# Reordering the seven block products of an FFN on one Trainium2 core: plain products first, weight sums fetched two blocks ahead, eight feature splits moved, one down block no longer halved

## The chip, the core and the metric

The kernel runs on one core of a Trainium2 chip. The core has TensorE (matrix products), VectorE and ScalarE (element-wise work), GpSimd (a few element-wise operations and some DMA issues) and SyncE, whose queue issues most DMAs. Traces abbreviate them as PE (with PEld for its weight loads), DVE, ACT, POOL and SP. Each engine has its own instruction stream; semaphores connect them. The metric is device microseconds of one execution of the whole program, the median of several runs.

## The reference, cut to what matters

The program is one layer of a streaming encoder for 512 tokens and width 1024: two parallel token mixers, cross-attention into 256 memory tokens, a SwiGLU FFN, a final RMSNorm. Only the FFN and the end are touched here:

```
gate, up = split(rmsnorm(x, norm_ffn) @ w_gate_up, (2816, 2816))
x = x + (silu(gate) * up) @ w_down
return rmsnorm(x, norm_final)
```

All data are float32. The kernel gets float32 accuracy from three products of a reduced format: an operand is split into a high part (one ScalarE copy, L111) and a low part (one VectorE subtraction, L113), and TensorE adds high·high, high·low and low·high.

## The kernel before, in words

The 2816 features are 22 blocks of 128, numbered j = 0 to 21. Blocks 0 to 2 are computed in the plain way, with two products over the full contraction of 1024 (gate, then up), 512 tokens wide. While they run, `ffn_sums` prepares for the others: it scales the input by its norm, cuts it into four quarters (contraction halves by token halves: b11, b12, b21, b22) and forms four combinations T1 to T4. Of the seven resulting activation tiles, named "11", "21", "22", "T1", "T2", "T3" and "T4", each is cut into four contraction pieces of 128 and split into high and low.

Blocks 3 to 21 are computed by `unit(j)` with seven products where the plain way has eight. The weights of gate and up make four quarters: a11 and a12 are the two contraction halves of the gate weights (one load into `raws[0]`), a22 is the second half of the up weights. Four sums of quarters are needed:

- s1 and s3 are formed by DMA: SyncE's queue loads the first half of the up weights twice (L1172), and GpSimd's queue adds a second quarter to each by an accumulating DMA (L1173, L1174).
- s2 = s1 + a11 and s4 = a12 + s2 are formed on VectorE (L1196, L1197), one after the other.

Every one of the seven weight operands goes through `quarter`: a high part by ScalarE into half of a `whi` buffer, a low part by VectorE into half of a `wlo` buffer. A product is 12 matmuls of 128x256 (four contraction pieces, three terms each), so a block is 84 matmuls. The order of the products before is a11·"11", s2·"T2", s1·"T1", s3·"T3", a12·"21", a22·"T4", s4·"22". VectorE combines the results out of PSUM by 128x256 operations (L1200 to L1217), ScalarE applies silu, and L1219 multiplies gate and up to one tile of the hidden layer.

Buffers that matter: tag "ti" has 4 tiles, "th" 4 tiles, `whi` and `wlo` 3 tiles each (two weight operands per tile), `raw` 3 tiles. Before, s1, s3 and s4 come from "ti" and s2, the gate tile `sg` and the result tile `cc` from "th".

The order of TensorE's instructions is the order in which the generators run: `drive` steps a unit by one contraction piece (three matmuls) and then steps everything in `pending`. The order on VectorE, ScalarE, GpSimd and SyncE is set at build time by a scheduler that sees program order and its own estimate of when inputs are ready; on the chip each engine then works through that fixed list.

The hidden tiles must themselves be split before the down projection (`gu_split`). Blocks 0 to 4 are split during units 10 to 14; before, the splits of blocks 5 to 21 are driven from the down stage, three of them ahead of it and the rest beside its first block. The down projection has 8 output blocks of 66 matmuls of 128x512. Before, blocks 0 to 5 are done that way; blocks 6 and 7 are done by token halves (128x256 matmuls, `wd_last`): both blocks for the left half, then both for the right half, so that the norm and the output of the left half (`final`) run beside the right half.

Of the kernel before, what the change touches and what calls it, by code (L numbers as in the profile page):

```python
# [9 lines left out]
F32R = mybir.dt.float32r  # L10
AF = mybir.ActivationFunctionType
ALU = mybir.AluOpType
# [28 lines left out]
def hybrid_block(  # L41
# [25 lines left out]
    def G(tag, name, dt=F32):  # L67
        return up.tile([P, T], dt, tag=tag, bufs=SLOTS[tag], name=nm(name))
# [6 lines left out]
    def TMP(name, tag, bufs=None, shape=(P, T), dt=F32, pool=None):  # L75
        return (pool or tp).tile(list(shape), dt, tag="t" + tag, bufs=bufs or TB[tag], name=nm(name))
# [116 lines left out]
    def wait(n):  # L193
        for _ in range(n):
            yield
# [505 lines left out]
    def seq(*gens):  # L701
        for g in gens:
            yield from g
# [410 lines left out]
    def ffn_sums():  # L1114

        for n in NB:
            B[n] = []
        for i in range(4):
            x = []
            for k in (i, i + 4):  # L1120
                t = TMP("xn", "th")
                nc.vector.scalar_tensor_tensor(out=t, in0=x3[k], scalar=gain(C_FFN, k), in1=stat["row3"],
                                               op0=ALU.mult, op1=ALU.mult)
                x.append(t)
                yield
            his = [G("a" if i < 2 else "b", "fh", F32R) for _ in range(4)]
            los = [G("a" if i < 2 else "b", "fl", F32R) for _ in range(4)]
            for at, n in enumerate(NB):
                o = lh if at % 2 == 0 else rh
                B[n].append((his[at // 2][:, o], los[at // 2][:, o]))  # L1130
# [25 lines left out]
    def quarter(src):  # L1156

        if held[1] % 2 == 0:
            held[0] = [wp.tile([P, KD, P], F32R, tag=t, bufs=3, name=nm(t)) for t in ("whi", "wlo")]
        o = slice(4 * (held[1] % 2), 4 * (held[1] % 2) + 4)  # L1160
        held[1] += 1
        hi, lo = (t[:, o, :] for t in held[0])
        split(hi, lo, src)
        return hi, lo

    def unit(j):
        raws = [wp.tile([P, KD, P], F32, tag="raw", bufs=3, name=nm("raw")) for _ in range(2)]
        a11, a12, a22 = raws[0][:, 0:4, :], raws[0][:, 4:8, :], raws[1][:, 0:4, :]
        s1, s3, s4, s2 = (TMP("fs", t).rearrange("p (k f) -> p k f", k=4) for t in ("ti", "ti", "ti", "th"))
        nc.sync.dma_start(out=raws[0], in_=w_g[j])  # L1170
        for s in (s1, s3):
            nc.sync.dma_start(out=s, in_=w_u[j][:, 0:4, :])  # L1172
        nc.gpsimd.dma_start(out=s1, in_=w_u[j][:, 4:8, :], accum_op=ALU.add)  # L1173
        nc.gpsimd.dma_start(out=s3, in_=w_g[j][:, 0:4, :], accum_op=ALU.add)  # L1174
        nc.sync.dma_start(out=a22, in_=w_u[j][:, 4:8, :])
        e, U = TMP("fe", "c"), TMP("fU", "c")
        W, sg, cc = TMP("fW", "c"), TMP("fg", "th"), TMP("fcc", "th")
        tt = nc.vector.tensor_tensor
        rot = [PM, PD, PS, PM, PD, PM, PD]

        def product(ps, w, act):
            hi, lo = w
            for k in range(4):
                xh, xl = B[act][k]
                o = ps[:, :H]
                nc.tensor.matmul(out=o, lhsT=hi[:, k, :], rhs=xh, start=k == 0, stop=False)  # L1186
                nc.tensor.matmul(out=o, lhsT=hi[:, k, :], rhs=xl, start=False, stop=False)  # L1187
                nc.tensor.matmul(out=o, lhsT=lo[:, k, :], rhs=xh, start=False, stop=k == 3)  # L1188
                yield

        def bank(i):
            return rot[i]("fp")
        p1 = bank(0)
        yield from product(p1, quarter(a11), "11")
        nc.scalar.activation(e[:, lh], p1[:, lh], AF.Copy)
        tt(out=s2, in0=s1, in1=a11, op=ALU.add)  # L1196
        tt(out=s4, in0=a12, in1=s2, op=ALU.add)  # L1197
# [8 lines left out]
        tt(out=U[:, rh], in0=U[:, lh], in1=q[:, lh], op=ALU.add)  # L1206
        tt(out=cc[:, rh], in0=W[:, lh], in1=q[:, lh], op=ALU.add)
        p = bank(4)
        yield from product(p, quarter(a12), "21")
        tt(out=e[:, lh], in0=e[:, lh], in1=p[:, lh], op=ALU.add)  # L1210
        nc.scalar.activation(sg[:, lh], e[:, lh], AF.Silu)
        p = bank(5)
        yield from product(p, quarter(a22), "T4")
# [3 lines left out]
        tt(out=W[:, lh], in0=W[:, lh], in1=p[:, lh], op=ALU.add)  # L1217
        nc.scalar.activation(sg[:, rh], W[:, lh], AF.Silu)
# [12 lines left out]
    def gu_splits(js):  # L1231
        for j in js:
            gu_split(j)
            yield
# [32 lines left out]
    def final(tok, sq):  # L1267
        yield from wait(6)
        ps = [PS("r4") for _ in range(2)]
        for i, q in enumerate([acc4[:, tok]] + sq):  # L1270
            for tt in range(2):
                nc.tensor.matmul(out=ps[tt][:, 0:1], lhsT=q[:, tt * P : tt * P + P], rhs=ones[:, 0:1],  # L1272
                                 start=(i == 0), stop=(i == 2))
        var, rs = SM("r4", 2), SM("r4", 2)
        for tt in range(2):
            nc.vector.tensor_scalar(out=var[:, tt : tt + 1], in0=ps[tt][:, 0:1], scalar1=1.0 / D, scalar2=EPS,  # L1276
                                    op0=ALU.mult, op1=ALU.add)
        nc.gpsimd.tensor_tensor(out=rs, in0=var, in1=mhalf[:, :2], op=ALU.pow)  # L1278
        yield from wait(4)
        pr = PS("row4")  # L1280
        for tt in range(2):
            nc.tensor.matmul(out=pr[:, tt * P : tt * P + P], lhsT=rs[:, tt : tt + 1].to_broadcast([P, P]), rhs=ident,  # L1282
                             start=True, stop=True)
        for i in (3, 0, 1, 2):
            x = x2t[i][:, :, tok]
            nc.vector.tensor_tensor(out=x, in0=x, in1=pr[:, :H].unsqueeze(1).to_broadcast([P, 2, H]), op=ALU.mult)  # L1286
            (nc.scalar if i in (0, 2) else nc.sync).dma_start(out=outT[i][:, :, tok], in_=x)

    wd = series(w_d, dps, gu, wd_after, range(KD - 2), kt=KF, pieces=PIECES)
    side = gu_splits(range(5, KF))  # L1290
    for _ in range(3):
        next(side)
    drive(wd[0], side=side)
    drive(*wd[1:])
    for hf in range(2):
        tok, sq = slice(hf * H, hf * H + H), []
        drive(*[(wd_last(j, tok, PM("wd"), sq), None) for j in (KD - 2, KD - 1)])
        pending.append(final(tok, sq))
    flush()

# [71 lines left out]
```

## Time and profile before

| | us |
|---|---|
| median of 3 runs | 1235.74 (1234.57 to 1238.3) |
| the profiled execution, its time | 1235.55 |
| the profiled execution, first to last instruction (span) | 1233.8 |
| TensorE busy | 1202.9 (97% of the span) |
| VectorE busy | 765.7 (62%) |
| ScalarE busy | 585.4 (47%) |

The span is what the trace shows; the time of the same execution is 1.75 us longer, and all sums are made on the span. In a row of the timeline the first number is the start in us from the span's start, the second the duration; what stands in brackets is the engine's idle time before that row and the instruction that ended it. In a row of the windows the first number behind the stretch is its length, then the busy time of PE, PEld, DVE, ACT and POOL with the count of instructions, the clock granted to TensorE as a share of full speed, the DMA share and GB/s.

### The profile page before, as it was taken

How to read it: one execution, taken by the hardware profiler on the slowest of the kernel's cores; microseconds unless marked ns; L12 is line 12 of the kernel's file. 1: busy time of each engine (PE TensorE's matmuls, PEld its weight loads, DVE VectorE, ACT ScalarE, POOL GpSimd, SP SyncE). 2: the span in 40 equal slices, each digit the busy share in tenths (PEclk: the TensorE clock that was granted, in tenths of full speed). 3: DMA queues.
4: the chain of work that ended last, by engine and by line, in shares of the span. 5: the costliest groups of instructions: out<-in, count | busy, mean ns of one | idle time of the engine just before them, and what ended most of it. 6: DMA issues, size and time to landing. Idle time of an engine off the chain costs nothing. (4 is left out here: it accounts for less than half of the span.)

```text
span 1233.8 us, 19731 instructions
## 1 busy us (share of the span) xinstructions
PE 1202.9 (97%) x7571; PEld 1051.2 (85%) x7571; DVE 765.7 (62%) x1564; ACT 585.4 (47%) x1207; POOL 143.5 (12%) x143
## 2 busy tenths in 40 slices
PE   8999999999999999999999999999989989999997
PEld 8888887899998887777788998888789989988887
DVE  5967872356543488775365564455978878892234
ACT  7573333365741377665324443443544545462332
POOL 0022230220110000000022200003011111100000
PEclk9999998999999999999999999999989999999999
DMA  7253342211343432233324462113167766743343
GB/s 277 87 180 105 118 125 82 94 53 61 112 135 131 162 111 77 86 96 103 120 86 138 138 211 89 66 48 107 43 154 184 185 163 172 181 130 99 94 120 120
DMA packets 73053, 149.28 MB, mean 121 GB/s; under 512 B 19040, under 2 KB 27648, under 8 KB 72960
## 3 DMA queue, kind: packets, MB, share of 16 engines
q1 hardware_dynamic: 66400, 137.02, 34.2%
q0 software_dynamic: 5472, 9.96, 5.0%
q8 instruction: 59, 0.97, 0.3%
q10 hardware_dynamic: 1088, 1.05, 0.2%
q14 instruction: 34, 0.28, 0.1%
HBM read 140.13 MB, written 7.88 MB: 120 GB/s over the span
## 5 line engine op out<-in xcount | busy, mean ns | idle before, releaser
L111 ACT ACTIVATE whi<-raw 128x1024 fp32r<-128x1024 f32 (+4 forms) x224 | 206.4, 926 | 309.8 <-PE g L138 80.8
L113 DVE TENSOR_TENSOR wlo<-raw,whi 128x1024 fp32r<-128x1024 f32 (+4 forms) x210 | 228.5, 1092 | 154.6 <-ACT whi L111 152.5
L1188 PE MATMUL fp<-fh,wlo 128*128 128x256 f32 x532 | 152.9, 287 | 3.9 <-DVE wlo L113 3.9
L1186 PE MATMUL fp<-fh,whi 128*128 128x256 f32 x532 | 152.5, 287 | 3.5 <-ACT whi L111 3.2
L1187 PE MATMUL fp<-fl,whi 128*128 128x256 f32 x532 | 152.1, 286 | 2.0 <-DVE fl L113 2.0
L1188 PEld LDWEIGHTS fp<-fh,wlo 128*128 128x128 f32 x532 | 103.7, 195 | 5.1 <-DVE wlo L113 4.8
L1186 PEld LDWEIGHTS fp<-fh,whi 128*128 128x128 f32 x532 | 103.8, 195 | 4.1 <-ACT whi L111 3.6
L1187 PEld LDWEIGHTS fp<-fl,whi 128*128 128x128 f32 x532 | 103.8, 195 | 2.3 <-DVE fl L113 2.2
L111 ACT ACTIVATE whi<-fs 128x512 fp32r<-128x512 f32 x76 | 46.7, 627 | 63.5 <-PE fp L1187 46.3
L203 POOL TENSOR_TENSOR acc<-acc,sq 128x512 f32<-128x512 f32 x19 | 31.1, 1635 | 264.2 <-issue 159.7
L162 PE MATMUL nat<-whi,hh 128*128 128x256 f32 x192 | 58.8, 306 | 0.4 <-DVE conv L391 0.4
L163 PE MATMUL nat<-whi,hl 128*128 128x256 f32 x192 | 54.9, 286 | 0.0
L164 PE MATMUL nat<-wlo,hh 128*128 128x256 f32 x192 | 54.9, 286 | 0.0
L113 DVE TENSOR_TENSOR wlo<-fs,whi 128x512 fp32r<-128x512 f32 x76 | 51.3, 686 | 5.7 <-ACT whi L111 5.3
L138 PE MATMUL g<-gul,whi 128*128 128x512 f32 x132 | 51.8, 393 | 1.9 <-DVE gul L113 1.9
L139 PE MATMUL g<-guh,wlo 128*128 128x512 f32 x132 | 51.5, 390 | 0.0
L137 PE MATMUL g<-guh,whi 128*128 128x512 f32 x132 | 51.5, 390 | 0.0
L799 ACT ACTIVATE P<-P,mx 128x128 f32<-128x128 f32 (+1 forms) x64 | 35.8, 559 | 28.7 <-DVE mx L797 28.5
L113 POOL TENSOR_TENSOR wlo<-raw,whi 128x1024 fp32r<-128x1024 f32 x14 | 34.0, 2428 | 111.3 <-ACT whi L111 111.3
L162 PEld LDWEIGHTS nat<-whi,hh 128*128 128x128 f32 x192 | 37.4, 195 | 1.5 <-issue 0.6
L1173 POOL DMA_DIRECT2D fs<-in_w_u x19 | 16.7, 877 | 181.8 <-DVE wlo L113 82.2
L163 PEld LDWEIGHTS nat<-whi,hl 128*128 128x128 f32 x192 | 37.5, 195 | 0.0
(416 smaller groups left out, 3328.3 us busy)
## 6 DMA issues: line engine op xcount, KB each, us to landing
raw<-in_w_g SPq DMA_DIRECT2D x22, 512.0 KB, 5.7
raw<-in_w_d SPq DMA_DIRECT2D x20, 512.0 KB, 3.5
fs<-in_w_u SPq DMA_DIRECT2D x38, 256.0 KB, 3.7
fs<-in_w_u POOLq DMA_DIRECT2D x19, 256.0 KB, 4.0
fs<-in_w_g POOLq DMA_DIRECT2D x19, 256.0 KB, 6.3
raw<-in_w_u SPq DMA_DIRECT2D x19, 256.0 KB, 4.2
raw<-in_wk SPq DMA_DIRECT2D x8, 512.0 KB, 3.9
raw<-in_wga SPq DMA_DIRECT2D x8, 512.0 KB, 3.5
```

The costliest lines, as they stand in the source:

```text
L111: nc.scalar.activation(hi, src, AF.Copy, scale=1.0 if scale is None else scale)
L113: (eng or nc.vector).tensor_tensor(out=lo, in0=src, in1=hi.bitcast(F32), op=ALU.subtract)
L137: nc.tensor.matmul(out=ps[:, :w], lhsT=hi[:, k - a, :], rhs=xh[:, n], start=first, stop=False)
L138: nc.tensor.matmul(out=ps[:, :w], lhsT=hi[:, k - a, :], rhs=xl[:, n], start=False, stop=False)
L139: nc.tensor.matmul(out=ps[:, :w], lhsT=lo[:, k - a, :], rhs=xh[:, n], start=False, stop=last)
L162: nc.tensor.matmul(out=o, lhsT=xh[:, tok], rhs=hi[:, kw, :], start=(k == 0), stop=False)
L163: nc.tensor.matmul(out=o, lhsT=xl[:, tok], rhs=hi[:, kw, :], start=False, stop=False)
L164: nc.tensor.matmul(out=o, lhsT=xh[:, tok], rhs=lo[:, kw, :], start=False, stop=(k == KD - 1))
L799: nc.scalar.activation(pr, pr, AF.Exp, scale=-1.0, bias=mx, accum_out=rs[:, t : t + 1])
L1186: nc.tensor.matmul(out=o, lhsT=hi[:, k, :], rhs=xh, start=k == 0, stop=False)
L1187: nc.tensor.matmul(out=o, lhsT=hi[:, k, :], rhs=xl, start=False, stop=False)
L1188: nc.tensor.matmul(out=o, lhsT=lo[:, k, :], rhs=xh, start=False, stop=k == 3)
```

## The change

1. In `ffn_sums` the same 32 tiles are allocated in another order (all four contraction pieces of "11" and "21" first, then of "22" and "T1", then the rest), so that tag "a" holds the operands of "11", "21", "22" and "T1".
2. In `unit`, s1 and s3 alone stay in "ti" (two tiles of four per block), s2 and s4 both come from "th".
3. The order of the products becomes a11·"11", a12·"21", s4·"22", s2·"T2", s1·"T1", s3·"T3", a22·"T4". The combining operations are rearranged with it: gate left is now e + product "21" straight into `sg` (L1200 of the new file), and s2 and s4 (now L1202, L1203) are written in the program behind it.
4. The splits of hidden blocks 5 to 12 run inside the last unit; only blocks 13 to 21 remain beside the first down block.
5. Down block 6 is done 512 tokens wide like blocks 0 to 5; only block 7 is halved.

```
         for i in range(4):
...
-            his = [G("a" if i < 2 else "b", "fh", F32R) for _ in range(4)]
-            los = [G("a" if i < 2 else "b", "fl", F32R) for _ in range(4)]
             for at, n in enumerate(NB):
                 o = lh if at % 2 == 0 else rh
-                B[n].append((his[at // 2][:, o], los[at // 2][:, o]))
+                B[n].append([t[:, o] for t in tiles[i, at // 2]])
...
-        s1, s3, s4, s2 = (TMP("fs", t).rearrange("p (k f) -> p k f", k=4) for t in ("ti", "ti", "ti", "th"))
+        s1, s3, s2, s4 = (TMP("fs", t).rearrange("p (k f) -> p k f", k=4) for t in ("ti", "ti", "th", "th"))
...
-        p1 = bank(0)
-        yield from product(p1, quarter(a11), "11")
-        nc.scalar.activation(e[:, lh], p1[:, lh], AF.Copy)
+        p = bank(0)
+        yield from product(p, quarter(a11), "11")
+        nc.scalar.activation(e[:, lh], p[:, lh], AF.Copy)
+        p = bank(1)
+        yield from product(p, quarter(a12), "21")
+        tt(out=sg[:, lh], in0=e[:, lh], in1=p[:, lh], op=ALU.add)
+        nc.scalar.activation(sg[:, lh], sg[:, lh], AF.Silu)
         tt(out=s2, in0=s1, in1=a11, op=ALU.add)
         tt(out=s4, in0=a12, in1=s2, op=ALU.add)
-        p = bank(1)
+        q = bank(2)
+        yield from product(q, quarter(s4), "22")
+        p = bank(3)
         yield from product(p, quarter(s2), "T2")
         tt(out=U[:, lh], in0=e[:, lh], in1=p[:, lh], op=ALU.add)
-        p = bank(2)
+        p = bank(4)
         yield from product(p, quarter(s1), "T1")
         tt(out=W[:, lh], in0=U[:, lh], in1=p[:, lh], op=ALU.add)
-        q = bank(3)
-        yield from product(q, quarter(s3), "T3")
...
-        p = bank(4)
-        yield from product(p, quarter(a12), "21")
...
+        tt(out=sg[:, rh], in0=W[:, lh], in1=q[:, lh], op=ALU.add)
+        nc.scalar.activation(sg[:, rh], sg[:, rh], AF.Silu)
         p = bank(5)
+        yield from product(p, quarter(s3), "T3")
...
+        p = bank(6)
         yield from product(p, quarter(a22), "T4")
         tt(out=cc[:, lh], in0=U[:, rh], in1=p[:, lh], op=ALU.add)
-        p = bank(6)
-        yield from product(p, quarter(s4), "22")
...
         if 9 <= j < 14:
             pending.append(seq(wait(8), gu_splits([j - 9])))
+        if j == KF - 2:
+            pending.append(seq(wait(10), gu_splits(range(5, 9)), wait(8), gu_splits(range(9, 13))))
...
-    wd = series(w_d, dps, gu, wd_after, range(KD - 2), kt=KF, pieces=PIECES)
-    side = gu_splits(range(5, KF))
-    for _ in range(3):
-        next(side)
+    wd = series(w_d, dps, gu, wd_after, range(KD - 1), kt=KF, pieces=PIECES)
+    side = gu_splits(range(13, KF))
...
-        drive(*[(wd_last(j, tok, PM("wd"), sq), None) for j in (KD - 2, KD - 1)])
+        drive(*[(wd_last(j, tok, PM("wd"), sq), None) for j in (KD - 1,)])
```

The build puts VectorE's instructions in the following order. First VectorE before, from the fifth product of block 4 to the second product of block 5. Here fs_9204 and fs_9205 are s1 and s3 of block 5, fs_9207 and fs_9206 its s2 and s4, raw_9202 its gate weights; wlo rows are low parts, each waiting for its high part from ScalarE.

```order
L1210 TENSOR_TENSOR fe_9072<-fe_9072,fp_9148 128x256 [waits PE_49]
L1196 TENSOR_TENSOR fs_9207<-fs_9204,raw_9202 128x512 [waits DMASW4_49]
L113 TENSOR_TENSOR wlo_9257<-fs_9204,whi_9256 128x512 [waits Activation_49]
L113 TENSOR_TENSOR wlo_9257<-fs_9205,whi_9256 128x512 [waits DMASW5_49,Activation_49]
L1197 TENSOR_TENSOR fs_9206<-raw_9202,fs_9207 128x512 [waits DVE_49]
L1214 TENSOR_TENSOR fcc_9076<-fU_9073,fp_9165 128x256 [waits PE_49]
L113 TENSOR_TENSOR wlo_9221<-fs_9207,whi_9220 128x512 [waits Activation_49]
L1217 TENSOR_TENSOR fW_9074<-fW_9074,fp_9183 128x256 [waits PE_49]
L113 TENSOR_TENSOR wlo_9292<-raw_9202,whi_9291 128x512 [waits Activation_49]
L113 TENSOR_TENSOR wlo_9292<-raw_9203,whi_9291 128x512 [waits DMAHW1_49,Activation_49]
L1219 SCALAR_TENSOR_TENSOR gu_9200<-fcc_9076,fg_9075 128x512 [waits Activation_49]
L1200 TENSOR_TENSOR fU_9215<-fe_9214,fp_9239 128x256 [waits PE_49]
```

Before, both sums of block 5 and the low part of s2 stand ahead of the last products of block 4 being combined. Now the same place in the changed kernel, from the end of block 4 into block 5: fs_9204 is s1 of block 5, fs_9206 and fs_9207 are its s2 and s4, fp_9237 is its product "21".

```order
L1220 TENSOR_TENSOR fcc_9076<-fU_9073,fp_9184 128x256 [waits DVE_49,PE_49]
L1221 SCALAR_TENSOR_TENSOR gu_9200<-fcc_9076,fg_9075 128x512 [waits DVE_49,Activation_49]
L1200 TENSOR_TENSOR fg_9217<-fe_9214,fp_9237 128x256 [waits PE_49,Activation_49]
L1202 TENSOR_TENSOR fs_9206<-fs_9204,raw_9202 128x512 [waits DMASW4_49]
L1203 TENSOR_TENSOR fs_9207<-raw_9202,fs_9206 128x512 [waits DVE_49]
L113 TENSOR_TENSOR wlo_9258<-fs_9206,whi_9257 128x512 [waits Activation_49]
L113 TENSOR_TENSOR wlo_9258<-fs_9207,whi_9257 128x512 [waits Activation_49]
L113 TENSOR_TENSOR wlo_9291<-fs_9204,whi_9290 128x512 [waits Activation_49]
```

The two sums now stand behind L1200, which waits for TensorE's product "21" of the same block. This is the order in all odd blocks from 5 to 21 (in block 21 with splits of hidden tiles in between). In the even blocks from 4 to 20 the low part of s4 stands further back; here block 4, where fs_9064 and fs_9065 are s2 and s4, fs_9063 is s3 and raw_9061 holds a22:

```order
L1200 TENSOR_TENSOR fg_9075<-fe_9072,fp_9093 128x256 [waits PE_49,Activation_49]
L1202 TENSOR_TENSOR fs_9064<-fs_9062,raw_9060 128x512
L1203 TENSOR_TENSOR fs_9065<-raw_9060,fs_9064 128x512 [waits DVE_49]
L113 TENSOR_TENSOR wlo_9131<-fs_9064,whi_9130 128x512 [waits Activation_49]
L113 TENSOR_TENSOR wlo_9167<-fs_9063,whi_9166 128x512 [waits DMASW3_49,Activation_49]
L113 TENSOR_TENSOR wlo_9167<-raw_9061,whi_9166 128x512 [waits DMAHW5_49,Activation_49]
L113 TENSOR_TENSOR wlo_9095<-fs_9065,whi_9094 128x512 [waits Activation_49]
```

Three other low parts now stand between s4 and its own low part. TensorE in the same block, from the last matmul of product "21" (fp_9093) into product "22" (fp_9114), whose weights are the halves of whi_9094 and wlo_9095 that hold s4:

```order
L1190 MATMUL fp_9093<-fh_8637,wlo_9095 128x256
L1188 MATMUL fp_9114<-fh_8639,whi_9094 128x256 [waits PE_49,Activation_49]
L1189 MATMUL fp_9114<-fl_8640,whi_9094 128x256
L1190 MATMUL fp_9114<-fh_8639,wlo_9095 128x256 [waits DVE_49]
L1188 MATMUL fp_9114<-fh_8641,whi_9094 128x256
```

The product with s4 was the seventh of a block and is now the third; its first matmul waits for ScalarE's high part, its third for VectorE's low part.

More of the change, by code (lines that the diff above doesn't have):

```diff
@@ L1117, in ffn_sums @@
             B[n] = []
+        tiles = {}
+        for at in range(4):
+            for i in range(4):
+                tiles[i, at] = [G("a" if at < 2 else "b", n, F32R) for n in ("fh", "fl")]
         for i in range(4):
@@ L1192, in bank @@
             return rot[i]("fp")
-        p1 = bank(0)
-        yield from product(p1, quarter(a11), "11")
-        nc.scalar.activation(e[:, lh], p1[:, lh], AF.Copy)
+        p = bank(0)
[5 more added lines that the diff above has]
+        nc.scalar.activation(sg[:, lh], sg[:, lh], AF.Silu)
         tt(out=s2, in0=s1, in1=a11, op=ALU.add)
         tt(out=s4, in0=a12, in1=s2, op=ALU.add)
-        p = bank(1)
+        q = bank(2)
+        yield from product(q, quarter(s4), "22")
+        p = bank(3)
         yield from product(p, quarter(s2), "T2")
         tt(out=U[:, lh], in0=e[:, lh], in1=p[:, lh], op=ALU.add)
-        p = bank(2)
+        p = bank(4)
         yield from product(p, quarter(s1), "T1")
         tt(out=W[:, lh], in0=U[:, lh], in1=p[:, lh], op=ALU.add)
-        q = bank(3)
-        yield from product(q, quarter(s3), "T3")
-        tt(out=U[:, rh], in0=U[:, lh], in1=q[:, lh], op=ALU.add)
-        tt(out=cc[:, rh], in0=W[:, lh], in1=q[:, lh], op=ALU.add)
-        p = bank(4)
-        yield from product(p, quarter(a12), "21")
-        tt(out=e[:, lh], in0=e[:, lh], in1=p[:, lh], op=ALU.add)
-        nc.scalar.activation(sg[:, lh], e[:, lh], AF.Silu)
+        tt(out=sg[:, rh], in0=W[:, lh], in1=q[:, lh], op=ALU.add)
+        nc.scalar.activation(sg[:, rh], sg[:, rh], AF.Silu)
         p = bank(5)
+        yield from product(p, quarter(s3), "T3")
+        tt(out=U[:, rh], in0=U[:, lh], in1=p[:, lh], op=ALU.add)
+        tt(out=cc[:, rh], in0=W[:, lh], in1=p[:, lh], op=ALU.add)
+        p = bank(6)
         yield from product(p, quarter(a22), "T4")
         tt(out=cc[:, lh], in0=U[:, rh], in1=p[:, lh], op=ALU.add)
-        p = bank(6)
-        yield from product(p, quarter(s4), "22")
-        tt(out=W[:, lh], in0=W[:, lh], in1=p[:, lh], op=ALU.add)
-        nc.scalar.activation(sg[:, rh], W[:, lh], AF.Silu)
         nc.vector.scalar_tensor_tensor(out=gu_tile(), in0=cc, scalar=-1.0, in1=sg, op0=ALU.mult, op1=ALU.mult)
@@ L1272, in final @@
                 nc.tensor.matmul(out=ps[tt][:, 0:1], lhsT=q[:, tt * P : tt * P + P], rhs=ones[:, 0:1],
-                                 start=(i == 0), stop=(i == 2))
+                                 start=(i == 0), stop=(i == len(sq)))
         var, rs = SM("r4", 2), SM("r4", 2)
```

## The prediction, made before the changed kernel ran

> **What bounds the kernel now.** I read the page first, then TensorE's waits, then the FFN by windows and, where it loses time, row by row.
>
> ```profile
> span 1233.8 us, 19731 instructions
> PE 1202.9 (97%) x7571; PEld 1051.2 (85%) x7571; DVE 765.7 (62%) x1564; ACT 585.4 (47%) x1207; POOL 143.5 (12%) x143
> ```
>
> TensorE is busy nearly throughout, so the time is its work plus its waits. Its longest waits over the whole span:
>
> ```profile
> PE fp L1188 <- DVE wlo L113: 3.9, 4, 1.9
> PE fp L1186 <- ACT whi L111: 3.2, 2, 2.0
> PE fp L1187 <- DVE fl L113: 2.0, 1, 2.0
> PE g L138 <- DVE gul L113: 1.9, 3, 1.4
> ```
>
> The first three are the seven-product units (fp), the fourth is the way into the down stage. The units from their first matmul to the first of the down stage:
>
> ```profile
> 890.65 0.28 PE L1186 MATMUL fp<-fh,whi 128*128 128x256 f32 x1
> ...
> 1097.62 0.39 PE L137 MATMUL g<-guh,whi 128*128 128x512 f32 x1
> ```
>
> That is 206.97 us for 19 blocks. In steady running a matmul starts every 0.12 us (the first two rows of the next fence), so a block needs 84 x 0.12 = 10.08 and 19 need 191.5. The units lose 15.45 us in all. One of the two places where they lose it shows how:
>
> ```profile
> 1002.38 0.28 PE L1187 MATMUL fp<-fl,whi 128*128 128x256 f32 x1
> 1002.50 0.28 PE L1188 MATMUL fp<-fh,wlo 128*128 128x256 f32 x1
> 1003.97 0.39 PE L1186 MATMUL fp<-fh,whi 128*128 128x256 f32 x1 [1.18 <-ACT whi L111]
> 1004.19 0.28 PE L1187 MATMUL fp<-fl,whi 128*128 128x256 f32 x1
> 1006.37 0.58 PE L1188 MATMUL fp<-fh,wlo 128*128 128x256 f32 x1 [1.91 <-DVE wlo L113]
> ...
> 1001.96 0.69 DVE L113 TENSOR_TENSOR wlo<-fs,whi 128x512 fp32r<-128x512 f32 x1 [2.21 <-ACT whi L111]
> 1002.57 0.68 DVE L1196 TENSOR_TENSOR fs<-fs,raw 128x512 f32<-128x512 f32 x1
> ...
> 1004.43 1.29 DVE L113 TENSOR_TENSOR wlo<-raw,whi 128x512 fp32r<-128x512 f32 x2
> 1005.64 0.68 DVE L113 TENSOR_TENSOR wlo<-fs,whi 128x512 fp32r<-128x512 f32 x1
> ...
> 1003.28 0.63 ACT L111 ACTIVATE whi<-fs 128x512 fp32r<-128x512 f32 x1
> ```
>
> VectorE stood 2.21 us at one instruction, and the sum s2 (L1196) queued behind it came late. Then everything went in a chain: sum 1002.57 to 1003.25, high part on ScalarE 1003.28 to 1003.91, first matmul 1003.97; the low part had to wait for two others and ended at 1006.32, third matmul 1006.37. The engine takes its list in order. Behind the stall TensorE's granted clock is 0.50:
>
> ```profile
> 896.80:903.60 6.80, 5.31 (x23) 5.01 (x24) 4.28 (x10) 1.69 (x4) 1.81 (x2) 0.50 0.65 166
> 1006.10:1009.40 3.30, 3.03 (x14) 3.03 (x15) 1.24 (x4) 0.70 (x2) 0.86 (x1) 0.50 1.04 301
> ```
>
> From 1006.37 to 1009.40, 14 matmuls took 3.03 us instead of 14 x 0.12 = 1.68: the half clock cost another 1.35. At the start of the units it lasted 6.8 us, twice as long, so up to 3.4.
>
> **The change, term by term.** *The third product.* By the order on VectorE, s2 and s4 now stand behind L1200, which needs the block's product "21", and TensorE's very next product needs s4. Nothing covers this chain: TensorE's list has no other product to go on with. (Before, the sums stood three or more products ahead.) The pieces of the chain, beside those above:
>
> ```profile
> 905.12 0.28 PE L1188 MATMUL fp<-fh,wlo 128*128 128x256 f32 x1
> ...
> 905.44 0.42 DVE L1206 TENSOR_TENSOR fU<-fU,fp 128x256 f32<-128x256 f32 x1 [1.01 <-PE fp L1188]
> 905.78 0.42 DVE L1207 TENSOR_TENSOR fcc<-fW,fp 128x256 f32<-128x256 f32 x1
> ...
> 990.21 0.69 DVE L1196 TENSOR_TENSOR fs<-fs,raw 128x512 f32<-128x512 f32 x1
> 990.93 0.69 DVE L1197 TENSOR_TENSOR fs<-raw,fs 128x512 f32<-128x512 f32 x1
> ...
> 907.94 1.15 ACT L111 ACTIVATE whi<-fs 128x512 fp32r<-128x512 f32 x2
> 909.00 0.62 ACT L111 ACTIVATE whi<-raw 128x512 fp32r<-128x512 f32 x1
> ```
>
> From the start of a product's last matmul to the VectorE operation that reads it is 0.32 (905.12 to 905.44), the next operation follows 0.34 later, s4 follows s2 by 0.72, high parts follow each other by 0.53, low parts by 0.60 (1004.43 to 1005.64 for two). Count from the start of the last matmul of "21":
>
> - Odd blocks: L1200 at 0.32, s2 at 0.66, s4 at 1.38 to 2.07; its high part 2.10 to 2.73, TensorE's first matmul at 2.79. The low part of s2 at 2.04, that of s4 when its high part is there, 2.76 to 3.45; third matmul 3.50. Without a wait it would be at 3 x 0.12 = 0.36: 3.14 us lost.
> - Even blocks: the low parts of s2, s3, a22 at 2.04, 2.64, 3.24, that of s4 at 3.84 to 4.53 (its high part, fourth on ScalarE from 1.38, is there at 3.60); third matmul 4.58: 4.22 lost.
> - Block 21: the splits of three hidden tiles stand between; s4 at 2.46, its low part 4.26 to 4.95: 4.64 lost.
> - Block 3: "11" and "21" are covered better than before, but behind L1200 stand three rows of `ffn_sums`, then s2, another such row, s4 and two low parts: 0.34 x 4 to s2, 0.94 to s4, 1.38 to the start of its low part, 0.69, 0.05, so 4.4 from L1200, which VectorE reaches some 0.8 late because it still works through the last pieces: 5.2 lost.
>
> Sum of the stalls: 9 x 4.22 + 8 x 3.14 + 4.64 + 5.2 = 72.9. The bounds are narrow, since every piece has a row: about 62 if the low part of s4 were always next in turn (18 x 3.14 and 5.2), 80 with another 0.4 of waiting in each block.
>
> *The half clock.* Each of the 19 stalls is like the one at 1002.5, whose two idle pieces (1.18 and 1.91, with two matmuls between) were enough. Bounds: nothing, or 3.2 each (nearly the 6.8 us stretch). I take 1.6, near the 1.35 of the same kind of stall, a little up because the even blocks' stalls are longer: 30.4. The units then lose 72.9 + 30.4 = 103.3 where they lost 15.45: **+87.9**.
>
> The Trainium skill, page "TensorE: Matmul & The Clock Gate", section "HAM oscillation — how this bites in real kernels", gives the rule that only gaps in TensorE's work of over some 3.4 us bring it back to half speed. By that rule hardly any of the new stalls would, since the longest unbroken idle piece is about 3.4 (even blocks, 0.28 to 3.65); the trace differs, since at 1002.5 no idle piece was over 1.91 and the clock still fell to 0.50, and I go by the trace. The rule makes the second rival below.
>
> *Weight sums two blocks ahead* (s1 and s3 use half of "ti" each block). This removes what made VectorE stand at 1001.96; what it gains lies within the 15.45 already taken off. The two extra loads and two accumulating DMAs that now go out early (about 720 us) pass SyncE's and GpSimd's queues, which have room:
>
> ```profile
> 900.12 0.92 POOL L1173 DMA_DIRECT2D fs<-in_w_u  x1 [37.80 <-DMA fs<-in_w_u]
> ```
>
> GpSimd stood idle 37.8 us ahead of its next sum. Cost zero; if that cover were gone the first blocks would start some us later. All later loads have more time than before, since a block takes 15 us.
>
> *Eight splits in block 21.* Three of them lengthen its stall (counted). The rest runs beside its last five products, so the 1.9 us in front of the down stage (the row of g L138) goes: **-1.9**, from 0 to -2.7.
>
> *Down block 6 whole.*
>
> ```profile
> 1130.60 0.69 DVE L1254 TENSOR_TENSOR x<-g,x 128x512 f32<-128x512 f32 x1 [1.99 <-PE g L139]
> 1145.63 0.69 DVE L1254 TENSOR_TENSOR x<-g,x 128x512 f32<-128x512 f32 x1 [1.99 <-PE g L139]
> ...
> 1208.96 1.25 PE r L1272 x12
> ```
>
> A whole block takes 15.03; 132 matmuls of 256 columns at 0.12 take 15.8, so 0.75 is saved, and 4 of the 12 small matmuls of the first half's norm (1.25 us in the row), 0.25 on average of what they cost. The left half's norm now has 7.9 us of block 7 as cover instead of 15.8 and needs about 5 until its outputs are issued. **-1.0**, from -1.2 to +2 if those outputs hold up the last ones.
>
> **Sum.** 1233.8 + 87.9 - 1.9 - 1.0 = 1318.8 for the span, and 1.75 more for the execution's time as before (1235.55 against 1233.8; the median of the runs, 1235.74, is the same within 0.2): **1320 us**.
>
> **The rivals.**
>
> 1. *Two half-clock stretches per stall.* The half clock begins late in a stall, finds little work in its first stretch and stays, as at 896.8. For it: the even blocks' stalls of over 4 us. Against it: the one stall of the same kind had one stretch. 19 x 3.2 = 60.8 in place of 30.4: 1351.
> 2. *No half clock.* Then 30.4 less: 1290. The row of clock 0.50 behind 1006.37 speaks against it.
> 3. *Faster: VectorE gets to the sums in time.* The mechanism would be that VectorE starts L1202 and L1203 while L1200 still waits for "21"; it decides from the point where both sums are ready 2.1 us ahead of the end of "21". Then the unit's waits go nearly all (2 us at the start stay): 1235.55 - 13.4 - 1.9 - 1.0 = 1219. The inputs are there, thanks to the earlier fetch. Against it: at 1001.96 VectorE stood 2.21 us with the sum behind it and did not take it.
> 4. *The change doesn't do what it says*: the fetch ahead is nullified because s2 and s4 share four "th" tiles with `sg` and `cc`, and gain and loss cancel. Only a cost of stalls near 18 us, one us per block, would do that, a third of the shortest chain.
>
> **Chances.** Forecast (1300 to 1340) 0.62; rival 1 0.15; rival 2 0.14; rival 3 0.06; rival 4 or otherwise within the noise 0.02; slower by a few us for other reasons 0.01. A measurement here can tell 0.3% (3.7 us). Faster by more: 0.06; within: 0.02; slower: 0.92. The range takes in rivals 1 and 2, whose bounds are those of the half clock: 1287 to 1353.
>
> **What would show it.** TensorE's waits "fp <- ACT whi" and "fp <- DVE wlo" with about 18 entries each, some 2.5 to 3.4 and 0.4 to 0.8 us long; blocks 10.1 us long before, alternately about 15 and 16 now; L1200 waiting on TensorE in every block and L1202 right behind it; clock segments of 0.50 in every block, 3.4 us each; the first g matmul some 88 us later than 1097.6; the down stage 3 us shorter. The forecast is wrong if L1202 starts ahead of L1200's product, or if the granted clock stays at 1 through the units.

## The result: 1322.68 us, and the profile after

The changed kernel takes 1322.68 us (median of 4 runs, 1320.84 to 1325.7) against 1236.03 for the kernel before: a ratio of 1.0684, 95% interval 1.0638 to 1.073. The profiled execution has a span of 1319.8 us, where 1318.8 had been worked out. Ratios, here and in the table of the experiments, leave out one run, of 1233.53 us in the row "the same again", which was over 1.5% above the fastest of its kernel.

The head of the page, after:

```profile
span 1319.8 us, 19554 instructions
PE 1235.9 (94%) x7497; PEld 1075.6 (81%) x7497; DVE 772.0 (58%) x1560; ACT 585.2 (44%) x1202; POOL 144.9 (11%) x144
```

TensorE has 74 instructions fewer and shows 33 us more busy time: the same matmuls took longer, for the most part because of the half clock. Its longest waits (waited for: total, times, longest):

```profile
PE fp L1188 <- ACT whi L111: 59.3, 19, 4.4
PE fp L1190 <- DVE wlo L113: 4.2, 14, 0.5
```

There are 19 waits for 19 units, all at the first matmul of the third product. The two stages by windows (length, then busy time of PE, PEld, DVE, ACT, POOL, granted clock, DMA share, GB/s):

```profile
889.22:1186.80 297.58, 233.77 (x1598) 225.03 (x1597) 184.78 (x342) 107.98 (x209) 29.45 (x34) 0.86 0.46 112
1186.80:1319.80 133.00, 124.58 (x620) 105.69 (x618) 48.38 (x63) 40.71 (x53) 9.15 (x8) 0.97 0.34 102
```

The units take 297.6 us instead of 207.0, the down stage 133.0 instead of 136.2, and the units begin 1.4 us earlier: 90.6 - 3.2 - 1.4 = 86.0, the difference of the spans. One odd block (9), TensorE, VectorE and ScalarE from the timeline:

```profile
988.08 0.28 PE L1190 MATMUL fp<-fh,wlo 128*128 128x256 f32 x1
990.93 0.39 PE L1188 MATMUL fp<-fh,whi 128*128 128x256 f32 x1 [2.57 <-ACT whi L111]
991.15 0.38 PE L1189 MATMUL fp<-fl,whi 128*128 128x256 f32 x1
991.66 0.58 PE L1190 MATMUL fp<-fh,wlo 128*128 128x256 f32 x1
...
988.47 0.42 DVE L1200 TENSOR_TENSOR fg<-fe,fp 128x256 f32<-128x256 f32 x1 [1.73 <-PE fp L1190]
988.81 0.68 DVE L1202 TENSOR_TENSOR fs<-fs,raw 128x512 f32<-128x512 f32 x1
989.53 0.69 DVE L1203 TENSOR_TENSOR fs<-raw,fs 128x512 f32<-128x512 f32 x1
990.19 2.62 DVE L113 TENSOR_TENSOR wlo<-fs,whi 128x512 fp32r<-128x512 f32 x4
...
989.53 2.40 ACT L111 ACTIVATE whi<-fs 128x512 fp32r<-128x512 f32 x4 [0.18 <-DVE fs L1202]
```

VectorE stands 1.73 us at L1200 until product "21" is out, and only then come s2 and s4; TensorE waits 2.57 us for the high part of s4. In the even blocks the splits stand in another order; block 10:

```profile
1002.75 0.28 PE L1190 MATMUL fp<-fh,wlo 128*128 128x256 f32 x1
1006.43 0.38 PE L1188 MATMUL fp<-fh,whi 128*128 128x256 f32 x1 [3.41 <-ACT whi L111]
...
1007.40 0.39 PE L1190 MATMUL fp<-fh,wlo 128*128 128x256 f32 x1 [0.47 <-DVE wlo L113]
...
1004.85 1.29 DVE L113 TENSOR_TENSOR wlo<-fs,whi 128x512 fp32r<-128x512 f32 x2
1006.07 0.68 DVE L113 TENSOR_TENSOR wlo<-raw,whi 128x512 fp32r<-128x512 f32 x1
1006.67 0.68 DVE L113 TENSOR_TENSOR wlo<-fs,whi 128x512 fp32r<-128x512 f32 x1
...
1004.19 1.15 ACT L111 ACTIVATE whi<-fs 128x512 fp32r<-128x512 f32 x2 [0.19 <-DVE fs L1202]
1005.25 0.61 ACT L111 ACTIVATE whi<-raw 128x512 fp32r<-128x512 f32 x1
1005.77 0.61 ACT L111 ACTIVATE whi<-fs 128x512 fp32r<-128x512 f32 x1
```

Three high parts (s2, s3, a22) stand on ScalarE ahead of that of s4, and three low parts on VectorE.

To split the 297.6, take the prediction's own measure of a stall: from the start of the last matmul of "21" to the start of the third of "22", less the 0.36 that this takes without a wait. Over the 19 blocks it comes to 74.2, and another 0.3 is lost in block 3 ahead of "21". Behind the third matmul of "22" a block has 58 matmuls left, 6.96 us at 0.12; together they take 31.5 more than that. Not all of this is the half clock: in the run with 24 matmuls in each stall (below), where one stretch of half clock is left, the 18 blocks without it take 7.05 for this part, 0.09 more than 6.96, or 1.8 over 19 blocks. So the stalls cost 74.2 + 0.3 + 1.8 = 76.3 and the half clock 29.7, and 191.5 + 76.3 + 29.7 is the 297.6 of the row but for rounding.

| term (us on the span) | predicted | measured |
|---|---|---|
| stalls at the third product | 72.9 | 76.3 |
| half clock behind them | 30.4 (19 stalls of 1.6) | 29.7 (13 stalls with one stretch, 1.36 each; 6 with two, 2.0 each) |
| losses of before that go | -15.45 | -15.5 |
| down stage | -2.9 | -3.2 |
| start of the units | 0 | -1.4 |
| sum | +85.0 | +86.0 (difference of the spans) |

### The profile page after: what moved, and what is told of

It reads as the page before. It is cut to its first block, busy times and chain, and to the rows that moved or that the text cites. A ratio compares the mean times of both kernels' runs of the same rounds, so it can differ in the third digit from the quotient of the medians.

```text
span 1319.8 us, 19554 instructions
## 1 busy us (share of the span) xinstructions
PE 1235.9 (94%) x7497; PEld 1075.6 (81%) x7497; DVE 772.0 (58%) x1560; ACT 585.2 (44%) x1202; POOL 144.9 (11%) x144
## 5 line engine op out<-in xcount | busy, mean ns | idle before, releaser
L113 DVE TENSOR_TENSOR wlo<-raw,whi 128x1024 fp32r<-128x1024 f32 (+4 forms) x207 | 224.4, 1092 | 177.2 <-ACT whi L111 174.2
L1188 PE MATMUL fp<-fh,whi 128*128 128x256 f32 x532 | 167.4, 315 | 59.3 <-ACT whi L111 59.3
L1190 PE MATMUL fp<-fh,wlo 128*128 128x256 f32 x532 | 167.5, 315 | 4.4 <-DVE wlo L113 4.2
L1188 PEld LDWEIGHTS fp<-fh,whi 128*128 128x128 f32 x532 | 117.6, 221 | 63.2 <-ACT whi L111 63.2
L1189 PE MATMUL fp<-fl,whi 128*128 128x256 f32 x532 | 164.7, 310 | 0.0
L1190 PEld LDWEIGHTS fp<-fh,wlo 128*128 128x128 f32 x532 | 116.7, 219 | 9.1 <-DVE wlo L113 9.1
L1189 PEld LDWEIGHTS fp<-fl,whi 128*128 128x128 f32 x532 | 117.1, 220 | 0.3 <-DVE fl L113 0.2
L138 PE MATMUL g<-gul,whi 128*128 128x512 f32 x154 | 60.1, 390 | 0.0
L139 PE MATMUL g<-guh,wlo 128*128 128x512 f32 x154 | 60.1, 390 | 0.0
L137 PE MATMUL g<-guh,whi 128*128 128x512 f32 x154 | 60.1, 390 | 0.0
```

The source lines that it names most:

```text
L113: (eng or nc.vector).tensor_tensor(out=lo, in0=src, in1=hi.bitcast(F32), op=ALU.subtract)
L137: nc.tensor.matmul(out=ps[:, :w], lhsT=hi[:, k - a, :], rhs=xh[:, n], start=first, stop=False)
L138: nc.tensor.matmul(out=ps[:, :w], lhsT=hi[:, k - a, :], rhs=xl[:, n], start=False, stop=False)
L139: nc.tensor.matmul(out=ps[:, :w], lhsT=lo[:, k - a, :], rhs=xh[:, n], start=False, stop=last)
```

## The experiments

Units means the time from the first matmul of unit 3 to the first of the down stage, from the profiled execution of each run. "Stalls" and "other excess" are a plain count over all successive matmuls of the units: what the time from one start to the next has over 0.12 us, added up for those over 0.4 us (stalls) and for the others. The others are the half clock and intervals of about 0.22 right behind a stall. All time comparisons are with runs of the kernel before on the same chip.

| kernel | time, us | ratio to before (95%) | units | stalls | other excess |
|---|---|---|---|---|---|
| before | 1236.03 | | 207.0 | 10.9 | 4.6 |
| changed | 1322.68 | 1.068 (1.064 to 1.073) | 297.6 | 70.3 | 35.7 |
| sums written first | 1252.52 | 1.010 (1.005 to 1.016) | 225.7 | 23.4 | 10.8 |
| old product order | 1228.05 | 0.992 (0.990 to 0.995) | 202.4 | 8.1 | 2.7 |
| "22" last | 1297.68 | 1.043 (1.031 to 1.056) | 264.3 | 49.2 | 23.6 |
| 18 matmuls in each stall | 1300.77 | 1.052 (1.045 to 1.059) | 275.0 | 31.0 + 41.0 filled | 11.5 |
| 24 matmuls in each stall | 1298.03 | 1.046 (1.031 to 1.061) | 269.5 | 18.6 + 54.7 filled | 4.7 |
| before, two ahead only | 1230.46 (one run) | | 201.6 | 7.1 | 3.0 |
| "T1" third, "T2" fourth | 1221.62 | 0.988 (0.982 to 0.994) | 195.0 | 3.3 | 0.2 |
| the same again | 1224.79 | 0.982 (0.973 to 0.991) | 195.0 | 3.3 | 0.2 |
| "T2" third, "T1" fourth | 1220.95 | 0.982 (0.975 to 0.989) | 194.7 | 2.8 | 0.3 |

### The sums written first

```
+        tt(out=s2, in0=s1, in1=a11, op=ALU.add)
+        tt(out=s4, in0=a12, in1=s2, op=ALU.add)
         p = bank(0)
         yield from product(p, quarter(a11), "11")
...
         nc.scalar.activation(sg[:, lh], sg[:, lh], AF.Silu)
-        tt(out=s2, in0=s1, in1=a11, op=ALU.add)
-        tt(out=s4, in0=a12, in1=s2, op=ALU.add)
```

> The changed kernel, but the two weight sums s2 and s4 are written in the program at the head of the unit instead of behind the combination with product "21". Products, buffers, splits and the down stage stay. By the build's order the sums then stand among the last combinations of the block before; in the odd blocks the low part of s4 is also ahead of L1202 (the combination with "21"), in the even blocks its high part is still fifth on ScalarE behind the high parts of s3 and a22, which wait for a buffer that product "11" frees, and its low part stands behind L1202. Theory A (the sums' place behind the combination makes the stalls): odd blocks lose at most 0.3 us, even blocks about 1.6 (first matmul of "22" 0.9 late, third another 0.6), the clock stays at 1 in most blocks; units 213 us instead of 297.6, time 1237. Rival B (product "22" is late because its inputs arrive late by DMA or because its splits take their time, wherever the sums stand): stalls of about 3 us stay in every block, time above 1290.

Two lines in another place take 70 us off. Most odd blocks lose 0.05 to 0.07 us, most even ones about 2.0, so rival B falls: the inputs and the splits are early enough where the list lets them. VectorE in block 8 (even):

```profile
957.24 0.69 DVE L1196 TENSOR_TENSOR fs<-raw,fs 128x512 f32<-128x512 f32 x1
...
960.25 0.42 DVE L1202 TENSOR_TENSOR fg<-fe,fp 128x256 f32<-128x256 f32 x1
960.58 0.68 DVE L113 TENSOR_TENSOR wlo<-fs,whi 128x512 fp32r<-128x512 f32 x1
```

s4 is ready at 957.93, its low part still stands behind L1202. The time was missed by 15 us: block 3 loses 7.6, even blocks 2.0 instead of 1.6, blocks 10 to 12 another 5 (in block 12 a split of a hidden tile stands between L1202 and the low part of s4), and the clock falls in blocks 3, 4, 6 and 12.

### The old order of products

The unit's body is that of the kernel before, the operand tiles are named in its order ("11", "T2", "T1", "T3", "21", "T4", "22"); the rest is the changed kernel.

> The changed kernel with the unit's products in the order of before ("11", "T2", "T1", "T3", "21", "T4", "22") and the operand tiles named in that order; s1 and s3 two blocks ahead, the eight splits in block 21 and the whole down block 6 stay. Theory A (only the place of the sums and of product "22" costs): the units keep the loss at their start (about 9.5 us) and lose the stall at block 13, 202 us; the way into the down stage and the down stage stay as in the changed kernel (133.0 us from the first g matmul to the end); time 1227, faster than before by about 9. Rival B (the fetch ahead, with half of the ti tiles, or the splits in block 21 cost time themselves): the units take 207 or more and the time is 1235 or above.

202.4 and 1228.05, as theory A had it: 17 of the 19 blocks take 10.08 us. So nothing but the order of products and sums makes the changed kernel slower.

### "22" last, the sums where they are

```
-        q = bank(2)
-        yield from product(q, quarter(s4), "22")
-        p = bank(3)
+        p = bank(2)
         yield from product(p, quarter(s2), "T2")
...
+        p = bank(6)
+        yield from product(p, quarter(s4), "22")
```

> The changed kernel with only product "22" moved from third to last place (operand tiles named in that order); the sums stay behind the combination with "21". The third product is now "T2", whose weights s2 are one sum behind the combination where s4 was two. Theory A (a sum written behind the combination of the second product stalls the product that needs it by the length of its chain): from the last matmul of "21", L1200 at 0.32, s2 0.66 to 1.35, its high part to 2.01, first matmul of "T2" at 2.07; s4 stands between s2 and the low part, which ends at 2.72, third matmul 2.77; 2.4 us lost in every block, odd and even alike, and the clock falls in most of them for 1.4 more: blocks of 12.5 to 14 us, units 235 to 262, time 1258 to 1285. Rival (only the two sums of s4 one after the other are too long, a single sum is hidden): blocks of 10.1 to 10.5, units 195 to 203, time 1219 to 1227.

The stall moved to the new third product, and is as long as its shorter chain (block 9):

```profile
977.43 0.28 PE L1190 MATMUL fp<-fh,wlo 128*128 128x256 f32 x1
979.55 0.38 PE L1188 MATMUL fp<-fh,whi 128*128 128x256 f32 x1 [1.85 <-ACT whi L111]
...
977.81 0.42 DVE L1200 TENSOR_TENSOR fg<-fe,fp 128x256 f32<-128x256 f32 x1 [1.35 <-PE fp L1190]
978.15 0.68 DVE L1202 TENSOR_TENSOR fs<-fs,raw 128x512 f32<-128x512 f32 x1
```

First matmul at 2.12 (2.07 expected), 2.4 to 2.6 us lost in most blocks. The units came out just above the upper end (264.3 against 262): blocks 3 and 21 lose over 6 us each. The time did not: the two runs took 1288.51 (the profiled one) and 1306.85, 3.5 and 22 us above the upper end. The mean granted clock of the slower one was 0.959 against 0.976, so it had more half clock; it has no trace that shows where. The rival falls: one sum behind the combination is enough.

### Matmuls that fill the stall

```
+        wt = quarter(a12)
-        yield from product(p, quarter(a12), "21")
+        yield from product(p, wt, "21")
...
         q = bank(2)
+        for _ in range(18):
+            nc.tensor.matmul(out=q[:, :H], lhsT=wt[0][:, 0, :], rhs=B["21"][0][0], start=True, stop=True)
         yield from product(q, quarter(s4), "22")
```

> The changed kernel with 18 extra matmuls of 128x256 between products "21" and "22" of every unit (high part of a12 times the first piece of "21", into the PSUM bank that product "22" then starts afresh), so that TensorE works 18 x 0.12 = 2.2 us of each stall. They end before the first weights of s4 are there (2.85 us after the last matmul of "21" in odd blocks, 3.69 in even ones), so the stalls themselves stay. Theory A (the stalls bring the half clock, and it costs 35.7 us): the stretches of clock 0.50 in the units go from 19 to 3 or fewer, the units shrink from 297.6 to about 263 us, time 1288. Rival (the half clock is not set off by idle time of this length, or costs nothing because the following products have room): time 1320 or, with the extra work on the path, above.

342 extra matmuls make the kernel 22 us faster than the changed one. The stalls are as long as ever: in every block the third matmul of "22" starts as far behind the last of "21" as in the changed kernel, within 0.02 us. The clock is at 0.97 over the units:

```profile
889.92:1164.96 275.04, 249.88 (x1939) 241.93 (x1938) 184.34 (x343) 108.15 (x209) 29.45 (x34) 0.97 0.50 121
```

The units were missed by 12 us for two reasons. Five stretches were left where at most 3 had been expected; they cost 7.1 us behind the third matmuls. And the 263 had put the whole "other excess" of 35.7 down to the clock, of which some 6 belong to the stalls. The same with `range(24)`:

> As the run with 18 extra matmuls per unit, but with 24 (2.9 us of TensorE work in each stall). Theory A (a stretch of 3.41 us in which TensorE works less than about half is followed by half clock): with 18, six stretches fell, all behind a window with a busy share of 0.49 or less; with 24 the idle left is 0 to 0.5 in odd blocks and 0.7 plus 0.6 in even ones, so no window but those of blocks 3 and 21 comes below 0.6, and at most 2 stretches of half clock are left. The stalls stay 72 us (filled or not), the units come to 191.5 + 72 + 1 to 4 = 265 to 268 us instead of 275, the time to 1290 to 1293. Rival (the half clock comes from something else in these blocks, such as the change of products): 5 or more stretches again, time near 1300 or above.

(The "six stretches" of this text were five.) One stretch is left in the units:

```profile
895.24:1164.75 269.51, 255.68 (x2054) 249.37 (x2052) 184.07 (x342) 108.18 (x209) 29.48 (x34) 0.99 0.51 124
901.56:904.97 3.41, 1.79 (x13) 1.59 (x13) 3.31 (x7) 3.10 (x6) 0.00 (x0) 1.00 0.23 77
904.98:908.39 3.41, 3.41 (x19) 3.41 (x18) 1.66 (x4) 0.64 (x2) 0.92 (x1) 0.50 0.88 252
```

The second row is the emptiest window, the third the half clock behind it. Block 10, with the extra matmuls between the first two rows:

```profile
998.62 0.28 PE L1190 MATMUL fp<-fh,wlo 128*128 128x256 f32 x1
1002.31 0.39 PE L1188 MATMUL fp<-fh,whi 128*128 128x256 f32 x1 [0.54 <-ACT whi L111]
1002.53 0.28 PE L1189 MATMUL fp<-fl,whi 128*128 128x256 f32 x1
1003.28 0.39 PE L1190 MATMUL fp<-fh,wlo 128*128 128x256 f32 x1 [0.47 <-DVE wlo L113]
```

The third matmul of "22" starts 4.66 behind the last of "21", where it took 4.65 without the filling. So the filling leaves the stall as it is and takes away what stood behind it: the units are 28.1 us shorter than the changed kernel's, though they hold 456 matmuls more. The stretch that is left costs about 1.5 us, and 28.1 + 1.5 is the price of the half clock that was given above; it is the same comparison, not a second one. The time did not follow all the way (1298.03, not 1290 to 1293): the units began at 895.2, 6 us late, for the reason in the last section.

### Two ahead alone, in the kernel before

```
-        s1, s3, s4, s2 = (TMP("fs", t) ... for t in ("ti", "ti", "ti", "th"))
+        s1, s3, s2, s4 = (TMP("fs", t) ... for t in ("ti", "ti", "th", "th"))
```

> The kernel before with one edit alone: s1 and s3 come from ti, s2 and s4 from th, so the weight sums by DMA are fetched two blocks ahead. Products, splits and the down stage are those of before. Theory A (the loss at block 13 came from a DMA sum that was late): the loss at the start of the units stays (about 9 us), that at block 13 (4.95 us) shrinks to 1.5 or nothing, those at blocks 5 and 15 go; units 201 to 203 us instead of 207, the down stage 136.2 us as before. Rival (the fetch ahead takes something from the blocks, since s4 now shares four th tiles with s2, the gate tile and the result tile): blocks over 10.1 us in the whole stage, units 207 or more.

Theory A: block 13 loses 1.5 instead of 4.95, blocks 5 and 15 nothing. This edit is worth 5.3 us of the units; in the changed kernel it can't be seen beside the stalls.

### Versions that are faster than both

The plain halves lead, the sums are written at the head of the unit, and the product with s4 is last. First with "T1" third:

```
         p = bank(2)
         yield from product(p, quarter(s1), "T1")
         tt(out=W[:, lh], in0=e[:, lh], in1=p[:, lh], op=ALU.add)
         p = bank(3)
         yield from product(p, quarter(s2), "T2")
         tt(out=U[:, lh], in0=e[:, lh], in1=p[:, lh], op=ALU.add)
         tt(out=W[:, lh], in0=W[:, lh], in1=p[:, lh], op=ALU.add)
...
         p = bank(6)
         yield from product(p, quarter(s4), "22")
```

> The changed kernel with the products in the order "11", "21", "T1", "T2", "T3", "T4", "22": the plain halves still lead, then the two products whose weights need no VectorE sum or only s2, and "22" with s4 last; the sums are written at the head of the unit; one more combination of 128x256 per block on VectorE. By the build's order every low part stands well ahead of its product. Theory A: all blocks from 4 on take 10.1 us, block 3 between 11 and 16; units 193 to 198 us, first g matmul near 1085, time 1217 to 1222, faster than before by some 15 us. Rival B (it is not the place of the sums but VectorE's load, with the extra operation, or the early leading halves that hold the units back): blocks of 11 us and more, time 1235 or above.

> The version with "T1" third and "T2" fourth once more, beside the one above on the same chip: units 195 us, time 1219 to 1224, faster than before by 12 to 16 us. If the gain were an accident of the earlier runs, the two would come out at the time of before.

Then with "T2" third, so that W = U + "T1" as before and the additional operation goes:

> As the version with "T1" third and "T2" fourth, but "T2" third and "T1" fourth, which saves the additional combination per block on VectorE; sums at the head of the unit. Theory A: in the build's order the low part of s2 stands ahead of the block's combination with "21" in odd and even blocks, so blocks of 10.1 us from 4 on; block 3 needs s2 two products earlier than there, while VectorE still works through the last pieces of the input, and loses 5 to 7 us instead of 3.5; units 196 to 199 us, time 1220 to 1224. Rival (the third product is too early for any sum formed in the same stretch): stalls of 1 us and more in each block, units above 210.

All three runs have 10.08 us in every block from 4 on. In the "T2" version the two sums of block 7, whose first matmul starts at 934.54, are formed around the end of block 6; the timeline, and the window of all units:

```profile
932.53 0.68 DVE L1195 TENSOR_TENSOR fs<-fs,raw 128x512 f32<-128x512 f32 x1
...
934.07 0.68 DVE L1196 TENSOR_TENSOR fs<-raw,fs 128x512 f32<-128x512 f32 x1
```

```profile
891.08:1085.74 194.66, 192.30 (x1597) 191.68 (x1596) 175.04 (x344) 105.41 (x208) 29.57 (x34) 1.00 0.70 171
```

Its block 3 loses 3.1 us, not 5 to 7. The two versions can't be told apart in time; both are 1.2 to 1.8% faster than before (the intervals reach from 0.6 to 2.7%) and some 100 us faster than the changed kernel. Both keep the idea of the change (plain halves first) and its other parts.

## Why the prediction was right, point by point

**What bounds the kernel.** TensorE, as said; every microsecond it waited showed in the time.

**The third product.** Right in place and cause, and 3.4 us short in size. In the odd block above L1200 starts 0.39 behind the last matmul of "21" (0.32 predicted), s2 at 0.73 (0.66), s4 at 1.45 (1.38), the first matmul at 2.85 (2.79), the third at 3.58 (3.50); in the even one the first at 3.68 (3.65), the third at 4.65 (4.58). The odd block's chain is 0.07 late from its first piece on. By the same measure block 3 loses 5.0 (5.2 predicted) and block 21 4.75 (4.64). In all it is 74.2 for the 72.9; the rest of the 76.3 is the 0.3 ahead of "21" in block 3 and the 0.09 behind the third matmul of each block, which the prediction did not count. That the list and nothing else holds the sums back is shown by the first experiment, that the length of the stall is that of the chain by the third.

**The half clock.** The mechanism was right, and the term came out at 29.7 for 30.4, in part by luck. In 13 stalls one stretch followed and cost 1.36 us on average, which is the 1.35 that the kernel before had shown; the even blocks' longer stalls account for little of the step to 1.6. Six stalls had a second stretch (rival 1 happened in blocks 3, 4, 6, 12, 20 and 21), at 2.0 us for the two, not 3.2. That 13 of the one kind and six of the other average near 1.6 was not foreseen. Rival 2 falls: with the stalls filled and just as long, the units are 28.1 us shorter. With it falls, for this kernel, the rule of the Trainium skill, page "TensorE: Matmul & The Clock Gate", section "HAM oscillation — how this bites in real kernels", "no PE-idle gaps >~3.4µs", taken to mean that shorter gaps do no harm: in the odd block an idle piece of 2.57 was enough, and in "22" last one of 1.85 in most blocks.

**Two blocks ahead.** Right: it costs nothing, and what it gains lay in the 15.45 already taken off; alone it is worth 5.3.

**Eight splits in block 21, down block 6 whole.** Down block 0 went from 17.75 to 15.03 us, -2.7, the far end of the range given (-1.9 predicted: only the waits had been counted, not the slow start of matmuls behind them). Blocks 6 and 7 went from 33.24 to 32.03, -1.2 (-1.0 predicted; its own rows give 15.84 - 15.03 = 0.81, not 0.75, and 4/12 of 1.25 = 0.4, not 0.25, together -1.2). Before, then after:

```profile
1097.62:1115.37 17.75, 15.89 (x68) 12.16 (x67) 13.44 (x20) 9.22 (x17) 0.00 (x0) 1.00 0.42 118
1190.50:1223.74 33.24, 33.24 (x280) 33.23 (x279) 15.57 (x20) 13.59 (x18) 2.00 (x2) 1.00 0.47 144
```

```profile
1186.80:1201.83 15.03, 15.03 (x69) 12.39 (x67) 12.54 (x20) 7.83 (x13) 0.00 (x0) 1.00 0.45 130
1276.97:1309.00 32.03, 32.03 (x211) 29.40 (x210) 12.27 (x16) 10.27 (x13) 3.29 (x3) 1.00 0.28 87
```

The tail behind them, from 1223.74 and 1309.00 to the end, grew from 10.1 to 10.8. The prediction had looked for a loss where the left half's outputs hold up the last ones. They did not: they had landed by 1311.0, and the first of the right half was issued at 1313.9. The four matmuls that write `row`, behind the norm's sum, start 2.94 and 2.93 us into the tail, but take 0.71 before and 1.15 after, at a granted clock of 0.55. Rows and windows before, then after:

```profile
1226.68 0.71 PE L1282 MATMUL row<-ident,r 128*128 128x128 f32 x4 [1.02 <-POOL r L1278]
1226.68:1227.39 0.71, 0.71 (x4) 0.52 (x4) 0.00 (x0) 0.00 (x0) 0.00 (x0) 1.00 0.00 0
```

```profile
1311.93 1.15 PE L1286 MATMUL row<-ident,r 128*128 128x128 f32 x4 [1.02 <-POOL r L1282]
1311.93:1313.08 1.15, 1.15 (x4) 0.86 (x4) 0.00 (x0) 0.00 (x0) 0.00 (x0) 0.55 0.00 0
```

That is 0.4 of the 0.7; the rest comes behind the issue of the last outputs, and its cause is open.

**Rivals 3 and 4.** VectorE never took a sum ahead of L1200, and the effect was nowhere near nothing. The 1.0 by which the sum was missed is made of the stalls (+3.4), the half clock (-0.7), the down stage (-0.3) and the start of the units (-1.4). That they nearly cancel was luck: nothing in the prediction foresaw the start of the units (next section but one).

## What to carry to other kernels

A sum that forms a weight operand must stand in its engine's list ahead of anything that waits for the product before it; VectorE worked its list in order in the traces shown here (it stood 1.73 us at L1200 with both sums queued behind it), so read the order that the build makes, not the program's. When products are reordered, ask of each operand that moves forward how long its chain is and how many products now cover it: here no product covered a chain of 3.6 to 4.7 us, and one product gives 12 x 0.12 = 1.44 us of cover. A stall that comes back in every block costs more than its length, because TensorE runs at half clock behind it; here that added 39% to it (29.7 to 76.3).

## What the runs showed of the hardware that was not expected

**Where the half clock begins.** The starts of the stretches in one trace lie whole multiples of 3.41 us apart (895.6, 912.7: five of them). Cut along these, what tells best is how much TensorE worked in a window, not one unbroken gap. In the run with the sums first:

```profile
911.64:915.05 3.41, 1.91 (x14) 1.50 (x14) 2.17 (x5) 1.11 (x3) 0.86 (x1) 1.00 0.68 172
915.05:918.46 3.41, 3.41 (x19) 3.41 (x18) 1.71 (x3) 1.15 (x2) 0.86 (x1) 0.50 0.98 229
...
1075.48:1078.89 3.41, 1.93 (x14) 1.72 (x15) 1.93 (x4) 0.92 (x3) 0.75 (x1) 1.00 0.88 264
1078.90:1082.30 3.40, 3.40 (x31) 3.40 (x30) 2.05 (x5) 1.09 (x2) 0.96 (x2) 1.00 0.93 202
```

Behind 1.91 us busy of 3.41 the next window had half clock (19 matmuls in it), behind 1.93 it did not (31 matmuls). In all eleven profiles, full-clock windows of the units with a busy share below 0.45 were always followed by it, those above 0.57 never, those between sometimes. The longest idle piece in a window tells less: 0.98 us of it was enough in the first row above, and 1.84 in a window of the changed kernel (from 1124.31) was not. So the same stall is dear or cheap by where it falls: in "22" last blocks with the same stall took 12.7 or about 14 us.

**A half clock under full load.** All runs but the changed kernel's have a stretch of half clock that begins near 195 us, long before the units, of 6.8 us in five profiles and longer in the others; in the first run with "T1" third it lasted 37.5:

```profile
194.80:232.30 37.50, 36.66 (x384) 32.64 (x384) 6.38 (x11) 7.89 (x15) 1.22 (x1) 0.50 0.05 16
```

TensorE was busy for 36.66 of it. The share that held in the units does not hold here: in the second run with "T1" third the window right ahead of its 6.8 us of half clock, with matmuls of 32x32 in it, has a busy share of 0.80:

```profile
191.62:195.03 3.41, 2.73 (x135) 2.29 (x135) 0.83 (x2) 2.50 (x8) 0.00 (x0) 1.00 0.58 219
```

The units of the execution with 37.5 us began at 902.8 where those of the second run began at 888.3, about half of the 30.7 us that its stretch is longer, and it took 1232.57 us where the other three runs took 1221 to 1222. In the run with 24 matmuls in each stall the stretch lasted 17.1 and the units began at 895.2. So it explains the late starts of the units in these profiles. The other runs have no trace, but each has a mean granted clock, and the times of the kernel before go with it: 1233.12 at 0.993, 1248 to 1250 at 0.976 to 0.979. Where their half clock lay can't be said, and why the stretch of 37.5 ends so late is open.
